# Rotating 96 images by 180 degrees: image groups taken every third image, and a longer last load piece

## The chip, the cores and the metric

The kernel runs on one core of one Trainium2 chip. The metric is the device time of one execution in microseconds (us); before the change the median of three runs is 122.17 us (122.12 to 122.32). The profile pages below come from one profiled execution, which has its own time. Instructions are named by their line in the kernel file (L47 is line 47). DVE is VectorE, ACT is ScalarE, SP is SyncE; SPq and ACTq are the instruction queues of SP and ACT, from which the DMA transfers are issued.

## The reference

```python
def setup_inputs():
    batch, c, h, w = 32, 3, 256, 256
    return {"x": np.random.randn(batch, c, h, w).astype(np.float32)}

def reference(x):
    return np.rot90(x, k=2, axes=(-2, -1)).astype(np.float32)
```

There are 32 x 3 = 96 images of 256 x 256 fp32 numbers, 256 KB each. A turn by 180 degrees reverses the order of the 65536 numbers of each image. So 25.17 MB are read, 25.17 MB are written, and each image is independent of the others.

## The kernel before, in words

An image is cut into four quarters of E = 16384 numbers (64 KB each). One quarter goes to one SBUF partition, so 32 images fill the 128 partitions: partition 4n+s holds quarter s of image n of the group. Three groups of 32 images make up the whole input, and each group has a tile of its own in SBUF: `A` (group 0), `Bt` (group 1) and `Ct` (group 2), 64 KB on each partition. Nothing is loaded twice and no tile is used again, so all loads can be issued at the start.

The work has three steps for each group.

- **Load.** `load` (L46, L47) brings a whole group with one DMA: `A` is issued on the SP queue (L66), `Bt` on the ACT queue (L67). The group `Ct` is loaded in three DMAs on the SP queue by `rows` (L62 to L64): the even partitions whole (L68), then the first E - LAST columns of the odd partitions (L69, called `ahead`), then the last LAST columns of the odd partitions (L70). LAST is 3072 numbers, 12 KB.
- **Reverse in SBUF.** `turn` (L72) calls `swap` (L53), which exchanges 2048 columns from the left with 2048 from the right in reversed order: three DVE copies (L44) through the scratch tile `T`. Four swaps, 12 copies, reverse a tile.
- **Store.** `store` (L49 to L51) writes a whole group with one DMA on the SP queue. The four quarters of each image are written in reversed order (`::-1` on the dimension s), which completes the turn.

The SP queue issues in program order: the load of `A`, the three loads of `Ct`, then the stores of `A`, `Bt` and `Ct`. A store waits for its tile's DVE copies. The first store has one wait more, put in by hand (L80 to L84): it is not issued before the transfer `ahead` has landed. At that point, of all the loads, only the last LAST columns of the odd partitions are still under way.

The transfers of the SP queue use DMA queue q1, those of the ACT queue use q10. Both are served by the same 16 DMA engines. A 64 KB row of a tile moves as one packet, so a full group is 128 packets, 8 for each engine; the 64 odd partitions of `Ct` give each engine four packets of 53248 B (`ahead`) and four of 12288 B (the last piece). Counted in bytes, each engine carries the equivalent of 24 packets of 64 KB for the loads and 24 for the stores.

The view `x4` (L29, L30) of the input says which images belong to a group. In it `(g n)` means that group g is the 32 images from 32g on, which lie in a row in memory; then `(n s)` can be folded into one dimension of 128 rows, 64 KB apart, and the DMA's pattern on the DRAM side has two levels: 128 rows of 16384 numbers. The view `o4` (L31, L32) of the output is grouped in the same way, but keeps n and s apart, because s is reversed; its pattern has three levels: 32 images, 4 quarters, 16384 numbers.

Of the kernel before, what the change touches and what calls it, by code (L numbers as in the profile page):

```python
# [2 lines left out]

os.environ.setdefault("NEURON_RT_ULTRASERVER_MODE", "4")

# [4 lines left out]


@with_exitstack
def kernel(
    ctx: ExitStack,
    tc: tile.TileContext,
    x: bass.AP,
    out: bass.AP,
):
    nc = tc.nc  # L20
    P = 128

    B, C, H, W = x.shape
    L = H * W
    G = 32
    E = L // 4
    J = E // 8

    x4 = x.rearrange("b c h w -> (b c) (h w)").rearrange(  # L29
        "(g n) (s e) -> g (n s) e", n=G, s=4)  # L30
    o4 = out.rearrange("b c h w -> (b c) (h w)").rearrange(  # L31
        "(g n) (s e) -> g n s e", n=G, s=4)  # L32

    pool = ctx.enter_context(tc.tile_pool(name="slots", bufs=1))
    A = pool.tile([P, E], x.dtype, tag="A")
    Bt = pool.tile([P, E], x.dtype, tag="B")
    Ct = pool.tile([P, E], x.dtype, tag="C")
    T = pool.tile([P, J], x.dtype, tag="T")

    def back(t, lo, hi):  # L40
        return t[:, hi - 1:(lo - 1 if lo else None):-1]

    def copy(dst, src):
        tc.keep_in_program_order(nc.vector.tensor_copy(out=dst, in_=src))  # L44

    def load(t, g, lo, hi, queue=nc.sync):  # L46
        return queue.dma_start(out=t[:, lo:hi], in_=x4[g][:, lo:hi])  # L47

    def store(t, g, lo, hi):  # L49
        return nc.sync.dma_start(  # L50
            out=o4[g][:, ::-1, lo:hi], in_=t[:, lo:hi])  # L51

    def swap(t, lo, w):  # L53
        hi = E - lo - w
        copy(T[:, 0:w], back(t, hi, hi + w))
        copy(t[:, hi:hi + w], back(t, lo, lo + w))
        copy(t[:, lo:lo + w], T[:, 0:w])

    half = E // 2
    LAST = 3072  # L60

    def rows(g, first, lo, hi):  # L62
        return nc.sync.dma_start(
            out=Ct[first::2, lo:hi], in_=x4[g][first::2, lo:hi])  # L64

    load(A, 0, 0, E)  # L66
    load(Bt, 1, 0, E, nc.scalar)  # L67
    rows(2, 0, 0, E)  # L68
    ahead = rows(2, 1, 0, E - LAST)  # L69
    rows(2, 1, E - LAST, E)  # L70

    def turn(t, lo, hi):  # L72
        while lo < hi:
            w = min(J, hi - lo)
            swap(t, lo, w)
            lo += w

    turn(A, 0, half)
    first = store(A, 0, 0, E)
    tc.add_manual_dep(  # L80
        first.ins, ahead.ins.name,
        mybir.DependencyInfo(
            mybir.DependencyClass.Sync, mybir.DependencyReason.DATA),
        reason="the first store waits for the loads' last columns but a few")  # L84
    turn(Bt, 0, half)
    store(Bt, 1, 0, E)
    turn(Ct, 0, half)
    store(Ct, 2, 0, E)


# [1 line left out]
_INS = ['x']  # L92
_OUTS = [((32, 3, 256, 256), 'float32')]


# [23 lines left out]
```

## Time and profile before

| what | value |
|---|---|
| median of three runs | 122.17 us (122.12 to 122.32) |
| the profiled execution, its own time | 122.16 us |
| its span (first to last instruction) | 120.4 us |
| around the span (122.16 - 120.4) | 1.76 us |
| DVE busy | 44.2 us (37%), 36 copies of 1226 to 1229 ns |
| share of 16 DMA engines' span, q1 and q10 | 81.2% and 16.1% |
| moved | 50.33 MB in 960 packets, 418 GB/s over the span |

The page of the profile gives busy time by engine, then the span in 40 equal slices (each digit is the busy share in tenths; the DMA row is the mean over the 16 engines), the DMA queues, and the DMA issues with the time from issue to landing. The view of one tile lists the instructions that touch it with their shortest, median and longest duration in ns. The view of windows cuts the span into stretches; in it a DMA packet is counted where it starts, so that a short stretch in which many packets start shows a share far above 1. Behind these views the trace holds one record for each DMA packet, with its queue, size, start and duration; where a text speaks of packets, it is from these records, with times counted from the span's start.

### The profile page before, as it was taken

The numbers are of one execution on the slowest core, as the hardware profiler recorded it, in microseconds if no ns is written. First come the engines' busy times: TensorE is split into PE (matmuls) and PEld (weight loads), VectorE is DVE, ScalarE is ACT, GpSimd is POOL, SyncE is SP. The second block draws the span as 40 slices with busy tenths as digits, with TensorE's granted clock in tenths as the row PEclk, the third lists the DMA queues.
The fourth block names the chain that finished last, engine by engine and source line by source line (L and its number), as shares of the span: only waits on it lengthen the run. The fifth ranks groups of instructions, "written<-read, shape, count | busy, mean of one in ns | idle before, by whom it ended". The sixth has DMA issues, their size and how long they took to land.

```text
span 120.4 us, 95 instructions
## 1 busy us (share of the span) xinstructions
DVE 44.2 (37%) x36; POOL 0.2 (0%) x4
## 2 busy tenths in 40 slices
DVE  0000000000000099999999999999900000000000
POOL 0000000000000000000000000000000000000000
DMA  9888988898889888979599888988898889888980
GB/s 348 348 348 348 697 348 348 348 675 370 348 348 675 370 348 348 596 318 548 238 389 697 348 348 348 697 348 348 348 697 348 348 348 697 348 348 348 675 370 0
DMA packets 960, 50.33 MB, mean 418 GB/s; under 512 B 128, under 2 KB 128, under 8 KB 128
## 3 DMA queue, kind: packets, MB, share of 16 engines
q1 hardware_dynamic: 816, 41.94, 81.2%
q10 hardware_dynamic: 144, 8.39, 16.1%
HBM read 25.17 MB, written 25.17 MB: 418 GB/s over the span
## 4 chain that ended last, share of the span: by engine, by line
DVE 37%; DMA 34%; issue 1%
DMA A<-in_x_dram 34%; DVE T L44 12%; DVE A L44 8%; DVE Bt L44 8%; DVE Ct L44 8%
## 5 line engine op out<-in xcount | busy, mean ns | idle before, releaser
L44 DVE COPY T<-A 128x2048 f32<-128x2048 f32 x4 | 4.9, 1226 | 42.1 <-DMA A<-in_x_dram 42.0
L44 DVE COPY T<-Ct 128x2048 f32<-128x2048 f32 x4 | 4.9, 1228 | 0.1
L44 DVE COPY A<-T 128x2048 f32<-128x2048 f32 x4 | 4.9, 1228 | 0.1
L44 DVE COPY Bt<-T 128x2048 f32<-128x2048 f32 x4 | 4.9, 1227 | 0.1
L44 DVE COPY A<-A 128x2048 f32<-128x2048 f32 x4 | 4.9, 1227 | 0.1
L44 DVE COPY T<-Bt 128x2048 f32<-128x2048 f32 x4 | 4.9, 1227 | 0.1
L44 DVE COPY Bt<-Bt 128x2048 f32<-128x2048 f32 x4 | 4.9, 1227 | 0.1
L44 DVE COPY Ct<-T 128x2048 f32<-128x2048 f32 x4 | 4.9, 1227 | 0.1
L44 DVE COPY Ct<-Ct 128x2048 f32<-128x2048 f32 x4 | 4.9, 1227 | 0.1
L103 POOL MEMSET const-bfloat16-1.0<- 128x1 bf16 x1 | 0.1, 102 | 0.0
L103 POOL MEMSET const-uint8-127<- 128x1 uint8 x1 | 0.1, 102 | 0.0
L103 POOL MEMSET const-float32-1.0<- 128x1 f32 x1 | 0.1, 99 | 0.0
L103 POOL MEMSET const-float32-0.0<- 128x1 f32 x1 | 0.1, 98 | 0.2 <-issue 0.2
## 6 DMA issues: line engine op xcount, KB each, us to landing
Ct<-in_x_dram SPq DMA_DIRECT2D x1, 3328.0 KB, 57.7
Ct<-in_x_dram SPq DMA_DIRECT2D x1, 768.0 KB, 58.9
A<-in_x_dram SPq DMA_DIRECT2D x1, 41.3
Bt<-in_x_dram ACTq DMA_DIRECT2D x1, 41.4
Ct<-in_x_dram SPq DMA_DIRECT2D x1, 50.5
out_dram<-A SPq DMA_DIRECT2D x1, 21.2
out_dram<-Bt SPq DMA_DIRECT2D x1, 28.0
out_dram<-Ct SPq DMA_DIRECT2D x1, 32.2
```

Source lines behind the costliest of these rows:

```text
L44: tc.keep_in_program_order(nc.vector.tensor_copy(out=dst, in_=src))
L103: nc = _bacc.Bacc("TRN2", target_bir_lowering=False, num_devices=1)
```

## The change

Two things are changed. First, the views of the input and of the output group the images differently: group g is now the images g, g+3, g+6 and so on, so that neighbours in a group are 768 KB apart in memory instead of 256 KB. The rows of such a group are no longer evenly spaced, so n and s cannot be folded in the view of the input: the loads' pattern on the DRAM side has three levels (32 images, 4 quarters, 16384 numbers), as the stores' pattern already had; for `rows` it is 32 images, 2 quarters and the columns. On the SBUF side nothing changes but a dimension of size 1. Second, LAST is 3392 numbers (13.25 KB) instead of 3072 (12 KB), so `ahead` is 12992 columns instead of 13312.

The bytes, the number of transfers, their order on each queue, all waits and all DVE copies are the same.

In the built programs the two full loads, of `A` and of `Bt`, differ in one more respect: before, their two instructions, and no other transfer's, carry a mark that the builder calls `ant_dge_precooked`; after, no transfer carries it.

```diff
     x4 = x.rearrange("b c h w -> (b c) (h w)").rearrange(
-        "(g n) (s e) -> g (n s) e", n=G, s=4)
+        "(n g) (s e) -> g n s e", n=G, s=4)
     o4 = out.rearrange("b c h w -> (b c) (h w)").rearrange(
-        "(g n) (s e) -> g n s e", n=G, s=4)
+        "(n g) (s e) -> g n s e", n=G, s=4)
...
     def load(t, g, lo, hi, queue=nc.sync):
-        return queue.dma_start(out=t[:, lo:hi], in_=x4[g][:, lo:hi])
+        return queue.dma_start(out=t[:, lo:hi], in_=x4[g][:, :, lo:hi])
...
     half = E // 2
-    LAST = 3072
+    LAST = 3392
 
     def rows(g, first, lo, hi):
         return nc.sync.dma_start(
-            out=Ct[first::2, lo:hi], in_=x4[g][first::2, lo:hi])
+            out=Ct[first::2, lo:hi], in_=x4[g][:, first::2, lo:hi])
```

## The prediction

> **What bounds the kernel now.** I read the page first, then the waits of SP's queue, then the single tiles for the durations of the issues, then windows around the change from loads to stores, and last the packet records. The page:
>
> ```profile
> span 120.4 us, 95 instructions
> ...
> DVE  0000000000000099999999999999900000000000
> ...
> DMA  9888988898889888979599888988898889888980
> ...
> q1 hardware_dynamic: 816, 41.94, 81.2%
> q10 hardware_dynamic: 144, 8.39, 16.1%
> ```
>
> DVE works in the middle alone; the DMA row is full from end to end, and its two queues fill 97.3% of the span of all 16 engines. The chain of waits on the page names DVE, but that work ends at 87.4 us and 33 us of stores follow. What sets the end is the 16 engines' packet streams. The waits of SP's queue confirm it:
>
> ```profile
> SPq L50 <- DMA Ct<-in_x_dram: 56.4, 1, 56.4
> SPq L114 <- DMA out_dram<-Ct: 19.3, 1, 19.3
> ```
>
> The first store is released by `ahead`'s landing, not by DVE (whose copies of `A` end at 57.1 us, 2.5 us earlier), and the program's end by the last store's. How long an issue takes, from the views of the tiles and of the output:
>
> ```profile
> L47 SPq DMA_DIRECT2D A<-in_x_dram x1: 386/386/386, 0.7 to 0.7; - x1
> ...
> L63 SPq DMA_DIRECT2D Ct<-in_x_dram x3: 569/596/689, 1.2 to 2.5; - x3
> ...
> L50 SPq DMA_DIRECT2D out_dram<-A x1: 623/623/623, 59.6 to 59.6; - x1
> L50 SPq DMA_DIRECT2D out_dram<-Bt x1: 562/562/562, 72.3 to 72.3; - x1
> L50 SPq DMA_DIRECT2D out_dram<-Ct x1: 539/539/539, 87.4 to 87.4; - x1
> ```
>
> The full load takes 386 ns to issue (as does `Bt`'s on ACT), every other transfer 539 to 689. The windows around the first store (columns: stretch, length, DVE, POOL, PE clock, DMA share, GB/s of packets starting there):
>
> ```profile
> 0.00:1.74 1.74, 0.00 (x0) 0.20 (x4) 1.00 0.00 0
> ...
> 60.40:60.60 0.20, 0.20 (x1) 0.00 (x0) 1.00 0.16 62
> 60.60:60.80 0.20, 0.20 (x1) 0.00 (x0) 1.00 0.02 0
> 60.80:61.00 0.20, 0.17 (x2) 0.00 (x0) 1.00 9.99 4260
> ```
>
> So there are two holes in the packet streams: 1.74 us at the start, and a short one near 60.7 us. The packet records (us from the span's start; 16 packets to a row, one of each engine):
>
> ```
> packets                     first start, last start   mean ns   last end
> A, first of each engine        1.741     2.472         3169      5.383
> 64 KB loads after that         4.883    48.877     2418 to 2420  51.295
> last piece, its fourth        60.061    60.522          460      60.982
> store A, first of each        60.889    61.054         2457      63.507
> 64 KB stores, 2nd to 24th     63.343   116.801     2420 to 2445  119.228
> ```
>
> Between the holes each engine runs its packets back to back: 65536 B in 2.42 us, 27.1 B/ns, whatever is loaded. 48 such packets are 116.2 us. The rest of the profiled 122.16 us is 1.74 before the first packet, 0.75 by which the first packets are longer, the hole, about 0.1 in longer stores, the skew between engines, and some 2.9 after the last packet, 1.76 of it outside the span. The profiled execution stands 0.01 below the median of 122.17, so the sum carries over.
>
> **The change part by part.**
>
> *Issue of `A`.* Its DRAM pattern gets a third level and the instruction loses the builder's mark; both then resemble the six slower issues. Nothing covers it: `A`'s first packet starts 0.62 us after its issue ends (0.73 + 0.386 = 1.12, to 1.74), and until then no engine has work. Store A behaves alike: 59.61 + 0.623 = 60.23, first packet 60.89, 0.66 later. So a longer issue moves every packet. Bounds: 0 (stays 386), and 689 - 386 = +0.30; a gain is excluded, as 386 is the shortest of the eight. I take store A's 623, the nearest row: 128 rows against a three-level pattern, on a queue that had long stood idle: +0.24. From issue to first packet the two differ by 1.28 - 1.01 = 0.27, which agrees.
>
> *Issues of `Bt` and the three `rows`.* `Bt`'s longer issue on ACT is hidden: its packets come second on every engine, from 4.88 us, and it would end near 1.36. The three issues on SP follow `A`'s 0.24 later and would end near 3.4 instead of 3.1; their packets start at 41 us. Cost nothing; the cover is 3.5 and 38 us.
>
> *LAST.* Per odd row 320 numbers, 1280 B, pass from `ahead` to the last piece: 47 ns at 27.1 B/ns, four rows an engine, so `ahead` lands 0.19 us earlier and store A's issue and first packets with it; the loads' total is unchanged. DVE does not take over as the late one (57.1 against 59.3). What it is worth is set by the engine that is latest. Now the last-piece packets end between 60.52 and 60.98, and the stores start between 60.89 and 61.05. After, the descriptors would be there by 61.05 - 0.19 = 60.86, but the latest engine is busy until 60.98 (60.99 with its 9 ns semaphore packet). So the latest store packet starts at 60.99 instead of 61.05: -0.07. The other engines gain up to 0.19, which doesn't set the end. Bounds: -0.19 if the latest engine were not the one, and +0.07, for one last-piece packet took 532 ns instead of 460, and more of them may meet the store's descriptors.
>
> *Stride.* Packets keep their size and number; only neighbouring images move from 256 to 768 KB apart. The loads of `A` and `Bt` (alternating, 8 MB apart) and those of half rows of `Ct` take the same 2418 to 2420 ns, so the addresses do not show in the time now. Bounds: a gain of at most 0.14 (24 stores from a mean of 2426 to 2420; the loads have no packet below 2418), and as a loss the slowest row of stores, 2445, for all: 25 ns x 24 loads + 19 x 24 stores = +1.1. I take 0, the value of the nearest rows.
>
> The Trainium skill speaks against the stride: in "DMA: Bandwidth & Descriptors", section "Latency and other measured facts", it tells of copies that slow down when rows lie a large power of two apart, with 207 GB/s at 512 KiB against 214 padded, and 103 at 4 MiB. In this trace images already lie 256 KB apart, at full pace, and no run yet shows 768 KB, which is no power of two; by the page's 512 KiB figure the sum would be an estimated 4 us more, near 126.
>
> *Launch.* Descriptors of `A` and `Bt` are made at the same time, and the engines start 0.73 us apart; store A's, made alone, 0.17 apart. The late starter's first packet is shorter (2911 against a mean of 3169), and it ends 0.29 after the mean (5.383 against 5.097). This skew may shrink with the new pattern (-0.29) or grow (+0.29, by the longest first packet, 3462). I take 0, for both queues still do the same.
>
> Sum: 122.16 + 0.24 - 0.07 = 122.33 us, +0.17 or 0.14%. About 0.2% (0.24 us) is what a measurement of this kernel tells from no change, so I forecast no measurable change, leaning to slower.
>
> **The rivals.**
>
> *Strided packets are longer (slower).* Place: every 64 KB packet, most likely the stores, which already vary. Beside the +0.17 it decides from 0.07 / 48 = 1.5 ns a packet; at 10 ns it gives 48 x 10 = 0.48, 122.8; at the bound above 123.4. For it: store rows of 2438 and 2445 ns exist. Against it: these two stand just after the issues of stores B and C (72.3 and 87.4), and the others are at 2420 to 2426.
>
> *The launch gets worse (slower).* Slower issues on two queues at once spread the engines' starts further: 122.33 + 0.29 = 122.62. For it: the three issues made back to back took up to 689. Against: store A's starts lie close together.
>
> *The launch gets better (faster).* The first packets, 16 of which begin 256 KB apart, lose their 0.75 us with the new spread of addresses: 122.33 - 0.75 = 121.58; half of it gives 121.96. For it: no later packet has this excess. Against: all first packets have it, so it looks like a filling of the path.
>
> *The issue costs nothing.* The new pattern issues in 386 ns as before, and only LAST remains: 122.16 - 0.07 to - 0.19, 121.97 to 122.09. For it: the first issue of a queue need not behave like later ones. Against: all six others are over 539.
>
> **How the numbers follow.** Forecast 0.42 (its own range 122.2 to 122.5: 0.34 within 0.2%, 0.08 slower); longer packets 0.26; worse launch 0.06; better launch 0.14 (0.12 faster, 0.02 within); no cost of the issue 0.12, all within. Together: faster 0.12, within 0.48, slower 0.40. For 8 in 10 the range goes from 121.9, which leaves out the better half of the better launch, to 123.0, which takes in longer packets up to 14 ns.
>
> **What the profile after would show.** The issue of `A` near 620 ns instead of 386, first packets near 1.98 us, `A` landing near 42.2; store A issued near 59.66 (59.61 + 0.24 - 0.19) while the last pieces still run, with the stretch free of packet starts gone; full packets at 2418 to 2420 (loads) and 2420 to 2445 (stores). The forecast is wrong if full packets are longer, if the first packets' excess or skew changes by over 0.1 us, or if `A`'s issue stays at 386.

## The result and the profile after

The changed kernel takes 122.56 us (median of 10 runs, 122.45 to 122.73), the kernel before 122.24 on the same chip (10 runs, 122.12 to 122.33). The ratio is 1.003, with a 95% interval of 1.0021 to 1.0039: 0.32 us slower, and the whole interval lies above the 0.2% that the prediction had called no change. The profiled executions say the same with the same sign: 122.45 us after (span 120.7) against 122.16 (span 120.4).

The page and the waits of SP's queue of the changed kernel:

```profile
span 120.7 us, 95 instructions
...
DVE  0000000000000089999999999999910000000000
...
DMA  9888998899889988999599888988898889888990
...
q1 hardware_dynamic: 816, 41.94, 80.4%
q10 hardware_dynamic: 144, 8.39, 16.7%
```

```profile
SPq L50 <- DMA Ct<-in_x_dram: 56.1, 1, 56.1
SPq L114 <- DMA out_dram<-Ct: 19.3, 1, 19.3
```

Nothing has changed its role: the DMA row is full from end to end, the first store is still released by `ahead`, the end by the last store. The shares of the two queues add up to 97.1% instead of 97.3%. What did change is in the issues (the views of the tiles `A`, `Bt` and `Ct` and of the output):

```profile
L47 SPq DMA_DIRECT2D A<-in_x_dram x1: 667/667/667, 0.7 to 0.7; - x1
...
L47 ACTq DMA_DIRECT2D Bt<-in_x_dram x1: 613/613/613, 0.7 to 0.7; - x1
...
L63 SPq DMA_DIRECT2D Ct<-in_x_dram x3: 603/615/819, 1.4 to 3.0; - x3
...
L50 SPq DMA_DIRECT2D out_dram<-A x1: 605/605/605, 59.7 to 59.7; - x1
L50 SPq DMA_DIRECT2D out_dram<-Bt x1: 572/572/572, 72.7 to 72.7; - x1
L50 SPq DMA_DIRECT2D out_dram<-Ct x1: 538/538/538, 87.9 to 87.9; - x1
```

The two full loads take 667 and 613 ns to issue, where both took 386. The issues of the stores are within 18 ns of those before. The windows show what this does to the start, and that the hole between loads and stores is no longer empty (columns: stretch, length, DVE, POOL, PE clock, DMA share, GB/s of the packets that start in it):

```profile
0.00:1.74 1.74, 0.00 (x0) 0.20 (x4) 1.00 0.00 0
1.74:2.04 0.30, 0.00 (x0) 0.00 (x0) 1.00 0.00 0
2.04:2.14 0.10, 0.00 (x0) 0.00 (x0) 1.00 0.00 0
...
60.40:60.60 0.20, 0.20 (x1) 0.00 (x0) 1.00 1.43 611
60.60:60.80 0.20, 0.20 (x1) 0.00 (x0) 1.00 0.64 271
60.80:61.00 0.20, 0.20 (x1) 0.00 (x0) 1.00 0.79 328
```

The second of these stretches in the kernel before is where most of its engines begin:

```profile
1.74:2.04 0.30, 0.00 (x0) 0.00 (x0) 1.00 8.76 2840
```

No packet starts before 2.14 us in the changed kernel. From there on the packet records of the two run in parallel, about 0.3 us apart (us from the span's start):

```
                                     before     after    shift
first packet of all                   1.741     2.140    +0.40
first packets, mean of 16 starts      1.928     2.256    +0.33
first packets, mean ns                 3169      3183
64 KB loads after that, mean ns   2418-2420  2418-2420
latest end of a load                 60.982    61.278    +0.30
store A, latest of 16 first starts   61.054    61.320    +0.27
stores, mean ns of all 384             2426      2426
last packet's end                   119.228   119.502    +0.27
```

So the time comes from the start of the packet streams. Of the 0.30 that the latest engine's loads are late, 0.03 come back at the hole between loads and stores. The 64 KB packets behind the first ones kept their length; the first ones took 14 ns more on average.

### The profile page after: what moved, and what is told of

The parts are those of the page before. It is cut to its first block, busy times and chain, and to the rows that moved or that the text cites. A ratio compares the mean times of both kernels' runs of the same rounds, so it can differ in the third digit from the quotient of the medians.

```text
span 120.7 us, 95 instructions
## 1 busy us (share of the span) xinstructions
DVE 44.2 (37%) x36; POOL 0.2 (0%) x4
## 4 chain that ended last, share of the span: by engine, by line
DVE 37%; DMA 35%; issue 1%
DMA A<-in_x_dram 35%; DVE T L44 12%; DVE Bt L44 8%; DVE A L44 8%; DVE Ct L44 8%
```

## The experiments

Two theories stood at the start. **I**: the loss is the longer issue of the full loads. **S**: it comes from the addresses, neighbouring images 768 KB apart. Beside them stood the question what the 1.25 KB more of LAST are worth. The diffs below are against the kernel before unless it says otherwise; times are medians, and each ratio is to the runs of the kernel before on the same chip.

### The mark alone

The prediction could not tell whether the third level of the pattern or the builder's mark makes an issue long. The builder can be told to leave the mark off:

```diff
+    nc.dge_precook = False
     load(A, 0, 0, E)
     load(Bt, 1, 0, E, nc.scalar)
```

> The kernel before with its groups, its two-level patterns and LAST 3072, but the builder's mark is taken from both full loads. Theory I (the whole loss is the longer issue of the full loads): their issues take 600 to 670 ns instead of 386, the first packet of all starts near 2.14 us instead of 1.74, and the time is 0.28 to 0.36 us above the kernel before. Theory S (the loss comes from the addresses 768 KB apart): the time is that of the kernel before within 0.1. Theory P (the third level of the pattern, not the mark, makes the issue long): issues stay at 386 and the time does not change.

Measured: 122.48 us against 122.24, ratio 1.0025 (1.0014 to 1.0035). The issues, from the views of the tiles `A` and `Bt`, and the start, from the windows:

```profile
L47 SPq DMA_DIRECT2D A<-in_x_dram x1: 579/579/579, 0.7 to 0.7; - x1
...
L47 ACTq DMA_DIRECT2D Bt<-in_x_dram x1: 528/528/528, 0.7 to 0.7; - x1
...
1.74:2.04 0.30, 0.00 (x0) 0.00 (x0) 1.00 0.00 0
2.04:2.14 0.10, 0.00 (x0) 0.00 (x0) 1.00 11.63 3932
```

With the old groups, the old pattern and the old LAST, the issues are 193 and 142 ns longer, the first packet starts at 2.055 us instead of 1.741, and 0.24 us of the 0.32 are there. Theory I holds for the larger part, and it does not need the third level (theory P falls); what the third level adds to an issue comes below. The measured 0.24 and the issues of 579 and 528 ns lie a little under what was expected.

### One mark of the two

```diff
+    nc.dge_precook = False
     load(A, 0, 0, E)
+    nc.dge_precook = True
     load(Bt, 1, 0, E, nc.scalar)
```

> The kernel before with the mark taken from the load of A (SP queue) alone; the load of Bt (ACT queue) keeps it. If the earlier of the two full loads sets when the engines begin, Bt's packets go first, from 1.74 us, A's second, and the time is within 0.1 of the kernel before. If it is A's issue that counts, as the prediction had it, the time rises by 0.25 to 0.35.

Measured: 122.17 us against 122.24, ratio 0.9996 (0.9984 to 1.0008). The issue of `A` on SP takes 582 ns, that of `Bt` on ACT 366:

```profile
0.00:1.74 1.74, 0.00 (x0) 0.20 (x4) 1.00 0.22 75
1.74:2.04 0.30, 0.00 (x0) 0.00 (x0) 1.00 7.92 2621
```

The first packet starts at 1.733 us, and in the packet records the first packets belong to `Bt`'s queue. A long issue of `A` costs nothing that these runs can show when `Bt`'s is short.

```diff
     load(A, 0, 0, E)
+    nc.dge_precook = False
     load(Bt, 1, 0, E, nc.scalar)
+    nc.dge_precook = True
```

> The kernel before with the mark taken from the load of Bt (ACT queue) alone. Both readings (earliest issue, or A's issue) expect A's packets first from 1.74 us and Bt's hidden behind them: within 0.1 of the kernel before. If Bt's issue is not hidden, the time rises by up to 0.3. It may also shrink the skew of the engines' starts (0.73 us before), if that comes from two sets of descriptors made at once: then down to 0.29 faster.

Measured: 122.23 us against 122.24, ratio 1.0 (0.9992 to 1.0009), with `A` issued in 377 ns, `Bt` in 519, and the first packet, `A`'s, at 1.729. So it is the earlier of the two full loads that starts the engines. The loss needs both to be slow, and in the changed kernel both are: there `Bt`'s packets go first, because its 613 ns end before `A`'s 667.

### The addresses alone

Here a tile's partitions hold every third quarter instead of every third image. Every fourth partition is then 768 KB further on, as in the changed kernel, but the 128 rows are evenly spaced, so the pattern keeps two levels and the loads keep their mark. The stores are those of the kernel before: the quarters are written to other places than the reference has them.

```diff
     x4 = x.rearrange("b c h w -> (b c) (h w)").rearrange(
-        "(g n) (s e) -> g (n s) e", n=G, s=4)
+        "n (s e) -> (n s) e", s=4).rearrange("(p g) e -> g p e", g=3)
```

> The kernel before, but a tile's partition p is loaded from quarter 3p+g of all quarters in a row: evenly spaced rows 192 KB apart, so every fourth partition is 768 KB on, as in the changed kernel, while the pattern has two levels and keeps the mark. The stores are those of the kernel before, so the quarters land in other places than the reference has them; bytes, packets and waits are the same. Theory I: issues at 386, first packet near 1.74 us, time within 0.1 of the kernel before. Theory S: slower by 0.3 or more, with longer packets or a longer start.

Measured: 122.26 us against 122.25, ratio 0.9998 (0.9989 to 1.0006). `A` is issued in 379 ns, the first packet starts at 1.734, the 64 KB loads take 2418 to 2420 ns. Theory S falls for the loads. For the stores 768 KB apart the changed kernel itself is the evidence: its 384 store packets have the same mean, 2426 ns, as the kernel before.

The Trainium skill ("DMA: Bandwidth & Descriptors", section "Latency and other measured facts") gives slower copies for rows a large power of two apart, 207 GB/s at 512 KiB. The prediction worked out 4 us from it as the price if it applied to 768 KB, which is no power of two. No such loss is in any of these runs: the loads and stores with images 768 KB apart keep the packet lengths above.

### LAST alone

```diff
-    LAST = 3072
+    LAST = 3392
```

> The kernel before with LAST 3392 alone. By the prediction's term: `ahead` lands 0.19 us earlier, the hole between loads and stores closes for the latest engine, and the time falls by 0.07 (between 0.03, what the changed kernel's profile shows from load end to store start, and 0.19). Rival: the larger last piece costs, because more of its packets meet the store's descriptors: up to 0.07 slower.

Measured: 122.19 us against 122.24, ratio 0.9993 (0.9985 to 1.0002). The sign may be right, but the interval holds no change. The rival's reason does not show: the packets of the longer last piece take 507 ns each, against 460 to 532 before, in step with their size. In the packet records the latest store A packet starts 0.047 us after the latest load's end, instead of 0.072: a gain of 0.025, not 0.07. The queue's descriptors do come earlier (store A is issued at 59.46 instead of 59.61, and its first packet starts at 60.740 instead of 60.889), but only engines that are early gain by it.

The same question from the other side, the changed kernel with LAST back at 3072 (diff against the changed kernel):

```diff
-    LAST = 3392
+    LAST = 3072
```

> The changed kernel with LAST back at 3072: the new grouping alone. Theory I: issues of the full loads as in the changed kernel (0.61 to 0.67), and the time 0.03 to 0.07 above the changed kernel, that is 0.35 to 0.40 above the kernel before; the full packets stay at 2418 to 2420 ns (loads) and 2420 to 2445 (stores). If LAST is what costs, the time falls back to that of the kernel before.

Measured: 122.77 us against 122.25, ratio 1.0043 (1.0028 to 1.0059). By the medians this made LAST worth 0.2 us in the changed kernel, against 0.05 in the kernel before, although the intervals of the two ratios (to 1.0039, and from 1.0028) overlap.

### Grouping and LAST, two by two on one chip

To settle this, the changed kernel, the changed kernel with LAST 3072, and the kernel before without the mark with either LAST ran on one chip. In the expectations, e1_mark_off is the run of the mark alone and e2_stride_only the changed kernel with LAST back at 3072; theory I+ is theory I with a further cost for the third level.

> The changed kernel again, beside the next three on one chip: a table of two by two, new grouping or old grouping without the mark, each with LAST 3072 and 3392. Expected 0.3 us above the kernel before. Theory I+: the mark costs 0.24 (e1_mark_off), the third level about 0.085 more (first packet 2.140 instead of 2.055 us), LAST gives 0.05 back: 0.24 + 0.085 - 0.05 = 0.28.

> The changed kernel with LAST 3072. Theory I+: 0.05 above the changed kernel, 0.33 above the kernel before. Rival (from the medians of e2_stride_only): LAST is worth 0.2 here, so 0.5 above the kernel before.

> The kernel before without the mark on both full loads, LAST 3072: 0.24 above the kernel before, as in e1_mark_off, and by theory I+ 0.085 below the changed kernel with LAST 3072. If the addresses cost something of their own, the distance is larger, 0.2 or more.

> The kernel before without the mark on both full loads, LAST 3392: theory I+ 0.05 below the same with LAST 3072 and 0.085 below the changed kernel. If LAST is worth 0.2 once the issues are long, it is 0.2 below and near the kernel before.

```
median us, ratio to 122.19 (95%)       LAST 3072                       LAST 3392
old groups, no mark              122.51 1.0018 (1.0009-1.0027)   122.53 1.0020 (1.0006-1.0033)
every third image                122.62 1.0034 (1.0022-1.0047)   122.69 1.0035 (1.0022-1.0048)
```

The ratios compare all runs and not only the two medians, so they are not the quotients of these. Across a row nothing changes by more than 0.07 us, and not with the expected sign. The 0.2 us of the earlier medians were not seen again, so LAST is worth nothing that these runs can show, in either kernel. Down a column the new grouping, with its third level, adds 0.11 to 0.16 us by the medians and 0.18 to 0.20 by the ratios. The records give part of it a place: the issues are 68 to 79 ns longer on both queues (647 and 612 against 579 and 533 with LAST 3392, 653 and 608 against 582 and 540 with 3072), and the first packet starts 0.07 to 0.08 later (2.128 and 2.134 against 2.054 and 2.059). Whether the rest is more than scatter stays open, for the intervals of the two rows overlap. The expectation had named 0.2 or more as the sign that the addresses cost something of their own. The times come too near to that to decide it; against it stand the packets, with 2419 ns for a load and 2426 for a store on average in all four kernels.

### The wait on `ahead` taken away

LAST sets how early the first store may be issued. The extreme is no such wait at all; the store then waits for DVE's copies of `A` only:

```diff
-    first = store(A, 0, 0, E)
-    tc.add_manual_dep(
-        first.ins, ahead.ins.name,
...
+    store(A, 0, 0, E)
```

> The kernel before without the first store's extra wait for `ahead`; it still waits for DVE's copies of A, which end at 57.1 us, so it is issued 2.4 us earlier. If the hole is worth what the latest engine loses in it, the time falls by 0.03 to 0.10. If all the engines' idle time in the hole counts (mean 0.25 us), it falls by 0.25. Rival: stores' descriptors made while loads still run disturb them, and the time rises.

Measured: 122.9 us against 122.25, ratio 1.0054 (1.0041 to 1.0068): slower by 0.65 us. The rival was right. The store's issue, and the windows of the same stretch, first without the wait:

```profile
L50 SPq DMA_DIRECT2D out_dram<-A x1: 623/623/623, 57.0 to 57.0; - x1
...
58.50:60.50 2.00, 1.97 (x2) 0.00 (x0) 1.00 0.96 221
```

then in the kernel before:

```profile
58.50:60.50 2.00, 1.97 (x2) 0.00 (x0) 1.00 0.91 387
```

The engines are as busy, but the packets that start there carry 221 GB/s instead of 387. The records say which: the 12288 B packets of the last piece take 681 ns on average and up to 1284, instead of 461. The latest of them ends at 62.053 us instead of 60.982, and the last store at 120.010 instead of 119.228, although the stores' own packets are shorter here (mean 2418 against 2426). The hole costs less than what fills it when the store is issued too early.

### `Bt` issued on SP too

```diff
-    load(Bt, 1, 0, E, nc.scalar)
+    load(Bt, 1, 0, E)
```

> The kernel before with the load of Bt issued on SP behind that of A, so only one set of descriptors is made at a time. If the 0.73 us between the engines' first starts come from two sets made at once, it shrinks towards store A's 0.17, the latest engine ends its loads earlier and the time falls by up to 0.29. If they do not, the time is within 0.1 of the kernel before. A lands near 22 us and DVE starts then, which does not set the end.

Measured: 122.21 us against 122.25, ratio 0.9997 (0.9989 to 1.0006). The engines' first starts are 1.02 us apart (1.734 to 2.750), not closer together, and the latest load ends at 60.992 against 60.982. So the engines' starts are as far apart with one issuing queue, and two sets of descriptors made at once are not needed for it. The Trainium skill says ("DMA: Bandwidth & Descriptors", section "Issuing engines are not separate DMA queues") that issuing from several engines only saves time on the sequencer; this run agrees, since moving the issue from ACT to SP moved the median by 0.04 us, no change within its interval.

### All of them by the start

```
                          issue ns   first    latest end   last packet's
                          A     Bt   packet   of a load    end
before                   386   386   1.741    60.982       119.228
LAST 3392                379   395   1.741    61.010       119.245
mark off A               582   366   1.733    61.014       119.286
mark off Bt              377   519   1.729    61.014       119.287
every third quarter      379   391   1.734    60.856       119.135
Bt on SP                 374   420   1.734    60.992       119.265
mark off both            579   528   2.055    61.201       119.471
 again                   582   540   2.054    61.311       119.566
 with LAST 3392          579   533   2.059    61.381       119.618
changed                  667   613   2.140    61.278       119.502
 again                   647   612   2.134    61.166       119.397
 with LAST 3072          647   612   2.131    61.543       119.765
 again                   653   608   2.128    61.276       119.531
```

The kernel without the wait on `ahead` is not in the table: its first packet starts at 1.751 us, but its loads end late for the reason above. The six kernels with at least one marked full load have their first packet by 1.741 us and the latest load's end at 60.86 to 61.01 (mean 60.98). In the seven profiles without a mark the first packet starts at 2.05 to 2.14, and the latest load ends at 61.17 to 61.54 (means 61.30 for the old groups and 61.32 for the new). The single profiles scatter by 0.1 to 0.2 us in the engine that comes last. None of the kernels tried is faster than the kernel before by more than its interval.

## Why the prediction was right or wrong

The range held the time, and the direction of the sum was right. Its forecast of no measurable change (122.33 us) was not right: the change is slower beyond 0.2%, an outcome that had 0.40 against 0.48.

- **What bounds the kernel.** Right. Packets keep their lengths, the first store hangs on `ahead`, and most of the shift of the first packets passes to the end.
- **Issue of `A`, +0.24.** This is the step that failed, by its size and by the load that it names. Right was the cause (the longer issue at the start, covered by nothing) and nearly the length of the issue: +0.28 for `A`. But not `A`'s issue counts, but the earlier of the two full loads, as one mark of the two showed: one short issue, of either load, brings the loss to nothing. What grew is therefore `Bt`'s issue (+0.23), and with it the time from the issue's end to the first packet: 0.62 before (1.116 to 1.741), 0.80 after (1.343 to 2.140). The prediction took 0.62 and 0.66 from two rows and held that time for fixed; without the marks alone, in the old pattern, it is 0.80 too. With both, the first packet is 0.40 later, the mean of the first starts 0.33, the latest load 0.30. That +0.24 lies near 0.30 is in part luck: it was taken from the issue that does not count, and it left out the 0.17 us by which the time behind the issue grew.
- **Issues of `Bt` and the `rows`, nothing.** Right for the `rows`. For `Bt` the named cover was that its packets come second; in the changed kernel they come first.
- **LAST, -0.07.** Not shown. The latest engine gained 0.03 in the changed kernel's profile and 0.025 in LAST alone, and the two-by-two shows nothing in the times. The reading that only the latest engine counts fits: in LAST alone the earliest engine got its store 0.15 us sooner and the end did not move.
- **Stride, nothing.** Right, by every third quarter for the loads and by the store packets' mean for the stores; by the times alone a small cost of the new grouping beyond the issues stays open. The rival of longer packets falls.
- **Launch, nothing.** The first packets' mean length stayed (3169, 3183). The engines' skew changes from run to run (0.38 to 1.25 us over these profiles) without a relation to the change. In the profiled pair it went from 0.73 to 0.39, beyond the 0.1 us that the prediction had named as a sign of being wrong; the same changed kernel, profiled again, had 0.87, so that bound was narrower than the scatter.

With +0.30 for the start and -0.03 for LAST, as the profiled pair shows them, the sum is +0.27. The profiled executions differ by 0.29, the medians by 0.32.

## What to carry to other kernels

In a kernel whose DMA engines are full from the first packet to the last, a delay of the first packet is paid about in full: here 0.31 us (the mark alone) came with 0.24 to 0.34 us more by the medians, and 0.39 to 0.40 (the new grouping) with 0.32 to 0.52. An access pattern's shape counts there even if bytes and packets stay as they are: with a regrouping that turned a two-level DRAM pattern into a three-level one, both first loads lost the builder's mark and its short issue. Here it was enough that one of the two queues which start together got its first transfer out quickly. Before crediting an earlier release, ask whether it moves the engine that comes last, and whether transfers queued early slow the small packets that still run.

## What the runs showed that was not expected

- From the issue's end to the first packet it takes 0.62 to 0.64 us when the earlier load has the mark, 0.79 to 0.80 when neither has it, and 0.65 to 0.66 for store A, except where it was issued without the wait on `ahead`; store A has no mark either, but is issued alone. Whether two unmarked issues at once make the difference was not tried.
- The 64-row load issued first behind the two unmarked full loads takes 819 to 841 ns of SP's queue, where it takes 569 in the kernel before; it is hidden here.
- A store queued behind small load packets, 2.6 us earlier than in the kernel before, stretched these packets from 461 to 681 ns on average, while the 53248 B packets just ahead of them hardly changed (1966 to 1971, the last of each engine). Why the small ones alone suffer was not found.
- In that same run the 384 store packets take 2418 ns on average, with no longer first packet, against 2426 in the kernel before. What the early issue saves there was not found either.
